# The experts' down product as three float32r matmuls with split weights, and two neighbouring weight rows to a partition

## The chip, the cores and the metric

The kernel runs on one core of a Trainium2 chip. The metric is the device time of one execution in microseconds (us), as the median of several runs. The engines are TensorE (PE in the profile, with its weight loads as PEld), VectorE (DVE), ScalarE (ACT), GpSimd (POOL) and SyncE (SP), which here issues most of the transfers.

## The reference, cut to what matters

One encoder layer over 1024 prompt and 256 sample tokens of 1024 features: two attentions, a gated merge, an output projection and a mixture of 32 experts, then a last norm. Everything is float32. The change lies in the experts:

```python
def hierarchical_moe(h, wg, bg, we, be, w1, w3, w2):
    ...
    def expert_block(args):
        xb, e = args
        return (jax.nn.silu(xb @ w1[e]) * (xb @ w3[e])) @ w2[e]
    ...
```

Each token goes to two of the 32 experts, so an expert has 80 tokens in the mean. `w1[e]` and `w3[e]` are 1024 x 512 and `w2[e]` is 512 x 1024, 2 MB each. The result is weighted, gated and added to the token's residual row.

## The kernel before

The expert stage takes the last third of the time. For each expert one block of up to 128 gathered token rows is worked on (`Block`): `xT` transposes the rows on TensorE, `up` makes the products with W1 and W3, `aT` transposes the activations, `down` makes the product with W2 and scatters the result back.

The loop over experts interleaves two experts on TensorE: the W1 product of expert e, the activation transposes of e - 1, the W3 product of e, the row transposes of e + 1, then the down product of e - 1. The order of the instructions on each engine is the order in which the program calls them, and each engine runs its own in order.

Products in float32r (a float32 rounded for one pass through TensorE) are made three at a time: high half by high half, low by high, high by low. For W1 and W3 `w_split` makes the halves of a 128 x 1024 quarter of the weights: ScalarE rounds it to the high half (line 1426), VectorE subtracts to get the low half (line 1427). The halves go to a ring of rooms of their own (`parts`, 2 * LEAD + 2 = 8 rooms of 4 KB a partition, four quarters). `w_next` hands out the next split quarter and has the one LEAD = 3 places further split. W2 isn't split: the down product reads the loaded quarters as float32 (line 1593), as it does the activations (`aT_`).

`w_load` loads a quarter from SyncE's queue into a free room, as far ahead as there are free rooms (`w_ahead`). Row r of a quarter of W1 or W3 goes to partition r mod 128, so a partition gets two runs of 2 KB, 128 rows apart; a W2 quarter has one row of 4 KB on each partition.

GpSimd issues the gather of the rows (line 1397) and the scatter that adds to the residual (line 1599). The rooms of `acts` hold a block's transposed rows and its output.

Of the kernel before, what the change touches and what calls it, by code (L numbers as in the profile page):

```python
# [10 lines left out]
F32 = mybir.dt.float32  # L11
# [22 lines left out]
class Slots:  # L34
    """4 KB rooms (1024 words a partition), given out in the order in which they fell free"""
# [4 lines left out]
    def ring(self, n):  # L40
        """n rooms set apart for one use"""
        return deque(self.free.popleft() for _ in range(n))
# [14 lines left out]
class Fm:  # L57
    """feature tiles of all tokens, chunk by chunk; rooms are taken when first touched"""
# [4 lines left out]
    def at(self, j, c, tok=None):  # L63
        """feature tile j of a chunk; tok: of one 128-token tile of it"""
        w = CHUNKS[c][1]
        per = 1024 // w
        o = (j % per) * w
        if (c, j // per) not in self.t:
            self.t[c, j // per] = self.s.get(self.dt)
        t = self.t[c, j // per]  # L70
        return t[:, o:o + w] if tok is None else t[:, o + tok * 128:o + tok * 128 + 128]
# [15 lines left out]
def kernel(ctx, tc, A, out_p, out_s, upto=99, dbg=None):  # L87
# [20 lines left out]
    def rsqrt(y, v, t):  # L108
        """y = v ** -0.5: square root and reciprocal, then a Newton step; t: room like y"""
# [6 lines left out]
    # scratch; a leading 2 where hi and lo parts lie side by side  # L116
# [40 lines left out]
    class Cols:  # L157
        """a group of up to 256 columns of w_in"""
# [29 lines left out]
    # column groups in the order of their use; gates only of the tokens behind the first chunk here  # L188
# [8 lines left out]
    # shift and scale of the first norm  # L197
# [36 lines left out]
    # norm statistics, then the normalised rows, transposed  # L234
# [46 lines left out]
    def ada0(hf):  # L281
# [12 lines left out]
        # norm_mix_g * (1 + scale): [p, hf, q, i, r], feature tile j = hf * 4 + q * 2 + i  # L294
# [17 lines left out]
    # the first column group runs feature tile by feature tile behind the modulation  # L312
# [30 lines left out]
    # the rest of the modulation, a piece at a time between projections  # L343
# [30 lines left out]
    def split_out(p, m, c, dst, row0, scale=1.0):  # L374
        """hi and lo of a PSUM (or SBUF) tile to scratch"""
# [13 lines left out]
    def work(g, *after):  # L389
        """the product with a loaded column group, then other parts; the next group's weights are split  # L390
        meanwhile, those of the one after are loaded"""
# [15 lines left out]
    def fm(g, evac, m=128, chunks=(0, 1, 2)):  # L407
        """feature-major column tile: out[m, tokens]"""
# [32 lines left out]
    # latents  # L441
# [69 lines left out]
    def rope(p, m, c, scale, dst, row0):  # L511
        """positions restart at the sample group"""
# [104 lines left out]
    def bias_out():  # L617
        """relative column bias of every query and key column"""
        SY.dma_start(tz_d, raw_ap(A["rpb"], 63, [[127, 120], [-1, 64], [1, 64]]))

    def bias_tables():
        """column bias of the neighbourhood attention by row distance, window-masked; the second table is of
        query tiles whose neighbourhoods lie inside the grid; a stage of each of three heads at a time"""
# [31 lines left out]
    class Piece:  # L655
        """[128, 8, 128] of weights: eight row tiles of 128 columns"""
# [24 lines left out]
    def piece_gates():  # L681
        """logits of the first chunk's gates"""
# [29 lines left out]
    class Merge:  # L712
        """per-branch projections and the gated merge, feature-major; the weights serve the first and the last
        chunk at once, then the middle one"""
# [95 lines left out]
    def fill(n):  # L810
        """up to the n-th product in all; a finished sum leaves its bank before the next begins"""
# [5 lines left out]
    def ktile(srcs):  # L817
        """a tile of hi or lo parts; srcs: (first partition, rows, dram)"""
# [6 lines left out]
    def heads(ap, rows, h0, nh, t0, w):  # L825
        """rows of each of nh heads, [rows, head, tokens]"""
        return ap[h0 * rows:(h0 + nh) * rows, t0:t0 + w].rearrange("(h d) n -> d h n", h=nh)

    class Job:
        """what a pair of heads (prompt) or two pairs (sample) need on chip"""  # L830
# [34 lines left out]
        def bias(b, h):  # L865
            if b.g:
                # two heads to a room, the rows that two query tiles reach
# [19 lines left out]
    class Unit:  # L887
        """a head's 128 queries"""
# [17 lines left out]
        def scores(u):  # L906
            """the score blocks, a bank each"""
# [34 lines left out]
        def transpose(u, b):  # L942
            """normalised P with the keys on partitions, in P's own place"""
# [12 lines left out]
    def pv(a, b):  # L956
        """both heads' values for one query tile"""
# [30 lines left out]
    for i in range(2):  # L988
# [5 lines left out]
        # two queries' pair of one kind, then of the other  # L994
# [48 lines left out]
    # logits = (x1 * rs * G2 + sh2) @ w + b = (x1 @ (G2 * w)) * rs + (sh2 @ w + b), features on partitions  # L1043
# [91 lines left out]
    # sum of the two column groups of the router's product  # L1135
# [30 lines left out]
    def rows_load(g):  # L1166
        """gate of the residual, shift, norm_ffn_g * (1 + scale), on all partitions"""
# [28 lines left out]
    # constants: column indices, token numbers (from 1), strict prefix matrix  # L1196
# [6 lines left out]
    # column indices less 64, so that the least number among zeros elsewhere is a column's  # L1203
# [6 lines left out]
    # of each token's two experts: number, place in the expert's list, weight  # L1210
# [231 lines left out]
    def w_next(e, m, q):  # L1442
        """the next quarter of the stream: of W1 and W3 split, LEAD quarters behind it are split before it is used"""
        if m == 2:
            return loaded.pop((e, m, q))
# [325 lines left out]
```

## Time and profile before

| what | before |
|---|---|
| median of 3 runs | 1901.58 us (1895.93 to 1902.13) |
| profiled execution, first to last instruction | 1893.6 us |
| TensorE busy | 1786.4 us (94%) |
| VectorE, ScalarE, GpSimd busy | 1034.4, 858.3, 328.9 us |
| expert stage in the profile | about 1235 to 1852 us |
| transfers in the expert stage | about 360 GB/s |

The time of a run also holds what lies before the first and after the last instruction; for the profiled execution itself only the span is known, and the runs lie 2.3 to 8.5 us above it. TensorE's busy time counts a matmul until its modelled end, so it overlaps with the next one's.

### The profile page before, as it was taken

The numbers are of one execution on the slowest core, as the hardware profiler recorded it, in microseconds if no ns is written. First come the engines' busy times: TensorE is split into PE (matmuls) and PEld (weight loads), VectorE is DVE, ScalarE is ACT, GpSimd is POOL, SyncE is SP. The second block draws the span as 40 slices with busy tenths as digits, with TensorE's granted clock in tenths as the row PEclk, the third lists the DMA queues.
The fourth block names the chain that finished last, engine by engine and source line by source line (L and its number), as shares of the span: only waits on it lengthen the run. The fifth ranks groups of instructions, "written<-read, shape, count | busy, mean of one in ns | idle before, by whom it ended". The sixth has DMA issues, their size and how long they took to land.

```text
span 1893.6 us, 28088 instructions
## 1 busy us (share of the span) xinstructions
PE 1786.4 (94%) x10298; PEld 1395.5 (74%) x10298; DVE 1034.4 (55%) x1739; ACT 858.3 (45%) x1392; POOL 328.9 (17%) x329
## 2 busy tenths in 40 slices
PE   5999999998999999989899999699999999999991
PEld 4777778997888888778688878566766667676760
DVE  6324422221455555444446566677777777777764
ACT  5313222221455555656633222265565656565642
POOL 0010210000222222222423100111111111111110
PEclk9999999999999999999999999799999999999996
DMA  9237787757632454755996553999999999999916
GB/s 352 92 113 214 239 277 219 225 167 209 141 100 63 118 155 120 218 156 157 272 312 205 189 211 132 347 340 369 365 365 361 354 366 353 364 356 367 348 37 238
DMA packets 294451, 453.85 MB, mean 240 GB/s; under 512 B 54711, under 2 KB 154119, under 8 KB 294311
## 3 DMA queue, kind: packets, MB, share of 16 engines
q1 hardware_dynamic: 277607, 403.77, 64.0%
q0 software_dynamic: 13824, 37.77, 7.2%
q10 hardware_dynamic: 2880, 10.49, 1.4%
q8 instruction: 83, 1.36, 0.3%
q14 instruction: 57, 0.47, 0.1%
HBM read 375.82 MB, written 90.67 MB: 246 GB/s over the span
## 4 chain that ended last, share of the span: by engine, by line
PE 85%; DVE 4%; DMA 4%; issue 3%; ACT 2%; SPq 1%; POOL 0%; DVEq 0%; POOLq 0%; ACTq 0%; another core or an unknown queue 0%
PE ph L1567 18%; PE pg L414 14%; PE py L1593 11%; PE s L918 6%; PE pw L1330 5%; PE fp L781 5%; PE o L968 5%; PE tp L950 5%; PE fp L693 4%; PE pg L576 3%; PE pt L1554 1%; PE pg L329 1%; PE pg L534 1%; DMA gate_d<-s 1%; DMA s<-nak_d 1%
## 5 line engine op out<-in xcount | busy, mean ns | idle before, releaser
L1567 PE MATMUL ph<-s,s 128*128 128x512 f32 x1536 | 377.9, 402 | 1.5 <-DVE s L1557 1.2
L1426 ACT CAST s<-s 128x1024 fp32r<-128x1024 f32 x256 | 265.9, 1055 | 195.0 <-PE ph L1567 195.0
L1567 PEld LDWEIGHTS ph<-s,s 128*128 128x128 f32 x1536 | 287.1, 189 | 73.9 <-issue 13.9
L1427 DVE TENSOR_TENSOR s<-s,s 128x1024 fp32r<-128x1024 f32 x256 | 304.6, 1222 | 64.5 <-ACT s L1426 55.2
L414 PE MATMUL pg<-s,s 128*128 128x512 f32 (+1 forms) x1488 | 284.5, 352 | 7.2 <-ACT s L176 6.0
L414 PEld LDWEIGHTS pg<-s,s 128*128 128x128 f32 (+1 forms) x1488 | 235.1, 186 | 57.5 <-ACT s L176 6.8
L1593 PE MATMUL py<-s,aT 128*128 128x512 f32 x512 | 225.1, 593 | 0.7 <-ACT aT L1582 0.7
L940 POOL TENSOR_SCALAR s<-s,m 128x1024 f32<-128x1024 f32 (+3 forms) x160 | 133.1, 832 | 472.1 <-DVE m L939 370.3
L1593 PEld LDWEIGHTS py<-s,aT 128*128 128x128 f32 x512 | 94.9, 190 | 108.1 <-issue 94.4
L918 PE MATMUL s<-s,s 96*128 96x512 f32 (+4 forms) x656 | 158.7, 365 | 1.4 <-ACT s L936 1.4
L936 ACT ACTIVATE s<-s,m 128x1024 f32<-128x1024 f32 (+3 forms) x160 | 135.1, 844 | 48.2 <-DVE m L926 27.2
L952 ACT COPY s<-tp 128x512 f32<-128x512 f32 (+1 forms) x160 | 86.7, 542 | 135.4 <-PE tp L950 132.8
L918 PEld LDWEIGHTS s<-s,s 96*128 96x128 f32 (+1 forms) x656 | 118.8, 190 | 27.3 <-ACT s L936 2.1
L950 PE MATMUL tp<-ident,s 128*128 128x128 f32 (+1 forms) x864 | 123.8, 276 | 11.4 <-POOL s L940 5.9
L693 PE MATMUL fp<-s,s 128*128 128x512 f32 x384 | 127.3, 432 | 0.3 <-ACT s L697 0.2
L950 PEld LDWEIGHTS tp<-ident,s 128*128 128x128 f32 (+1 forms) x864 | 101.7, 141 | 29.2 <-POOL s L940 10.6
L1330 PE MATMUL pw<-s,s 128*128 128x512 f32 x480 | 118.5, 402 | 0.0
L968 PE MATMUL o<-s,s 128*64 128x128 f32 (+1 forms) x1728 | 116.9, 281 | 0.2 <-ACT s L952 0.2
L177 DVE TENSOR_TENSOR s<-s,s 128x1024 fp32r<-128x1024 f32 (+1 forms) x32 | 38.3, 1200 | 143.2 <-ACT s L176 139.2
L781 PE MATMUL fp<-s,s 128*128 128x512 f32 (+1 forms) x576 | 112.4, 356 | 2.7 <-DVE s L670 1.0
L926 DVE TENSOR_REDUCE m<-s 128x1 f32<-128x1024 f32 (+1 forms) x80 | 85.0, 1062 | 51.3 <-PE s L918 50.8
L1599 POOL DMA_INDIRECT x_d<-s,idx x32 | 71.8, 2243 | 231.1 <-DVE s L1598 122.6
(227 smaller groups left out, 2041.7 us busy)
## 6 DMA issues: line engine op xcount, KB each, us to landing
s<-in_expert_w SPq DMA_DIRECT2D x384, 512.0 KB
s<-in_w_in SPq DMA_DIRECT2D x47, 512.0 KB
s<-in_ada_w POOLq DMA_DIRECT2D x32, 512.0 KB, 6.3
s<-nak_d SPq DMA_DIRECT2D x40, 256.0 KB
s<-in_x_prompt SPq DMA_DIRECT2D x16, 512.0 KB
s<-in_ada_w SPq DMA_DIRECT2D x16, 512.0 KB
s<-gate_d SPq DMA_DIRECT2D x16, 512.0 KB
gate_d<-s SPq DMA_DIRECT2D x16, 384.0 KB
```

The lines of the kernel that those rows point to most:

```text
L414: PE.matmul(p[:m, :CHUNKS[c][1]], g.at(a, j, 0, m), b.at(j, c), start=(j == 0 and n == 0), stop=(j == KD - 1 and n == 2))
L693: PE.matmul(p, w.at(a, j), b.at(j, 0), start=(n == 0), stop=(n == 23))
L781: PE.matmul(p[:, :w], b.ws[i].at(u, x * 4 + j), o[:, v, :w], start=(m == 0), stop=(m == 11))
L918: PE.matmul(u.s[:, b, :u.w], a, c, start=(n == 0), stop=(n == len(ops) - 1))
L936: S.activation(u.out, u.src, AF.Exp, bias=u.m[:, 0:1], scale=u.sign, accum_out=u.m[:, 1:2])
L950: PE.transpose(tp[:w, i // 128, :], u.P[:, b * 512 + i:b * 512 + i + w], ident)
L968: PE.matmul(o[64 * u.x:64 * u.x + 64, cs], u.job.vat(u.t0 + i // 128, u.h, w), v3(u.P, 8)[:w, i // 128, :], start=(i == 0), stop=(i + 128 ...
L1330: PE.matmul(b.p, x[b.c].at(k, b.c, b.k), w[:, k % 2, :], start=(k + i == 0), stop=(k == 7 and i == 2))
L1426: S.copy(hi, r)
L1427: V.tensor_sub(lo, r, f32(hi))
L1567: PE.matmul(p, a[:, 2 * q + k, :], v3(w, 2)[:, k, :], start=(q + k + i == 0), stop=(q == 3 and k == 1 and i == 2))
L1593: PE.matmul(p, b.aT_[:, k, :], w[:, hb * 512:hb * 512 + 512], start=(k == 0), stop=(k == 3))
```

## The change

The stream that `w_next` and `w_fill` walk through now holds the W2 quarters too: each is split like those of W1 and W3, with the subtraction on GpSimd (`G`) where it was on VectorE (`V`) for the others. `aT` makes a high and a low half of the transposed activations, in a room of `acts`, which has 4 rooms in place of 3. `down` makes three float32r matmuls for each quarter and half of the columns in place of one in float32; the third of the three reads the low half of the weights.

All loads now put row 2p and row 2p + 1 of a W1 or W3 quarter on partition p, one run of 4 KB. So that the rows of the gathered block meet the right weight rows, `xT` transposes every second column.

The loop for further blocks of experts with more than 128 tokens is changed in the same way; it makes no turn with these inputs. Comments and docstrings are left out of the new file, with the line numbers kept; they are left out here too.

```diff
-    LEAD, ACTS = 3, 3
+    LEAD, ACTS = 3, 4
...
-        SY.dma_start(v3(r, k), src.rearrange("(k p) n -> p k n", p=128)[:, q * k:q * k + k, :])
+        SY.dma_start(v3(r, k), src.rearrange("(q p k) n -> q p k n", p=128, k=k)[q])
         return r
 
-    def w_split(r):
+    def w_split(r, m):
         hi, lo = sl.get(F32R, parts), sl.get(F32R, parts)
         S.copy(hi, r)
-        V.tensor_sub(lo, r, f32(hi))
+        (V if m < 2 else G).tensor_sub(lo, r, f32(hi))
         sl.put(r)
         w_ahead(0)
         return hi, lo
 
     loaded, ready = {}, deque()
-    halves = [k for k in stream if k[1] < 2]
...
     def w_next(e, m, q):
-        if m == 2:
-            return loaded.pop((e, m, q))
-        assert halves[at[2]] == (e, m, q)
+        assert stream[at[2]] == (e, m, q)
         at[2] += 1
         w_fill()
         return ready.popleft()
 
     def w_fill():
-        while at[1] < min(len(halves), at[2] + LEAD):
-            ready.append(w_split(loaded.pop(halves[at[1]])))
+        while at[1] < min(len(stream), at[2] + LEAD):
+            ready.append(w_split(loaded.pop(stream[at[1]]), stream[at[1]][1]))
             at[1] += 1
...
                 for k in range(4):
-                    PE.transpose(p[:, k, :], b.xg[:, (hb * 4 + k) * 128:(hb * 4 + k) * 128 + 128], ident)
+                    o = (hb * 2 + k // 2) * 256 + k % 2
+                    PE.transpose(p[:, k, :], b.xg[:, o:o + 255:2], ident)
...
-            b.aT_ = ep.tile([128, 4, 128], F32, name="aT")
-            S.copy(b.aT_, p)
+            b.aHL = sl.get(F32R, acts)
+            b.aH, b.aL = [v3(b.aHL, 8)[:, 4 * i:4 * i + 4] for i in range(2)]
+            S.copy(b.aH, p)
+            V.tensor_sub(b.aL, p, f32(b.aH))
...
             for k in range(4):
-                w = quarter(2, k)
-                for hb, p in enumerate(ps):
-                    PE.matmul(p, b.aT_[:, k, :], w[:, hb * 512:hb * 512 + 512], start=(k == 0), stop=(k == 3))
-                sl.put(w)
-                w_ahead(0)
+                hi, lo = quarter(2, k)
+                for i, (a, w) in enumerate(((b.aH, hi), (b.aL, hi), (b.aH, lo))):
+                    for hb, p in enumerate(ps):
+                        PE.matmul(p, a[:, k, :], w[:, hb * 512:hb * 512 + 512], start=(k + i == 0), stop=(k == 3 and i == 2))
+                sl.put(hi, lo)
+            sl.put(b.aHL)
...
-        quarter = lambda m, q: w_split(raws[m, q]) if m < 2 else raws[m, q]
+        quarter = lambda m, q: w_split(raws[m, q], m)
```

## Rows read from the trace of the kernel before

**Rows 1.** The page: engines, busy us, share of the span, instructions.
```profile
PE 1786.4 (94%) x10298; PEld 1395.5 (74%) x10298; DVE 1034.4 (55%) x1739; ACT 858.3 (45%) x1392; POOL 328.9 (17%) x329
```
**Rows 2.** The chain that ended last, one expert: start us, us, what.
```profile
1435.21 6.87 PE py L1593 x16
1442.08 5.50 PE ph L1567 x24
1447.58 0.44 PE pt L1580 x4
1448.02 5.48 PE ph L1567 x24
1453.49 0.87 PE pt L1554 x8
```
**Rows 3.** Two stretches (engines' busy us, clock, DMA, GB/s); SP's wait, 1300 to 1780.
```profile
1550.00:1600.00 50.00, 50.00 (x192) 33.55 (x191) 36.08 (x38) 28.23 (x33) 10.02 (x6) 1.00 1.01 364
...
1815.00:1820.00 5.00, 5.00 (x24) 3.60 (x23) 5.00 (x6) 3.72 (x6) 0.00 (x0) 1.00 0.00 0
...
SPq L1421 <- DVE s L1427: 204.2, 197, 3.0
```
**Rows 4.** Groups by line, 1300 to 1800: busy us, mean ns of one, idle before.
```profile
L1427 DVE TENSOR_TENSOR s<-s,s 128x1024 fp32r<-128x1024 f32 x209 | 248.9, 1222 | 51.7 <-ACT s L1426 43.2 <-DMA s<-in_expert_w 5.0
L1426 ACT CAST s<-s 128x1024 fp32r<-128x1024 f32 x208 | 216.3, 1056 | 165.1 <-PE ph L1567 165.1
...
L1599 POOL DMA_INDIRECT x_d<-s,idx x26 | 59.9, 2304 | 172.3 <-DVE s L1598 92.8 <-DMA s<-h_d,idx 79.5
...
L1557 DVE TENSOR_TENSOR s<-pt,s 128x512 fp32r<-128x512 f32 x53 | 34.0, 683 | 0.0
L1588 DVE SCALAR_TENSOR_TENSOR s<-s,of,s 128x1024 f32<-128x1024 f32 x26 | 33.4, 1285 | 0.7
...
L1397 POOL DMA_INDIRECT s<-h_d,idx x27 | 28.0, 1037 | 248.1 <-PE pt L1554 248.1
...
L1572 ACT ACTIVATE a<-ph 128x512 f32<-128x512 f32 x26 | 15.5, 597 | 14.0 <-PE ph L1567 14.0
```
**Rows 5.** Groups by line of GpSimd over the whole span, the same columns.
```profile
L1354 POOL TENSOR_TENSOR s<-s,s 128x1024 f32<-128x1024 f32 x2 | 4.7, 2337 | 37.1 <-PE pr L1386 37.1
...
L520 POOL TENSOR_TENSOR s<-s 128x256 f32<-128x256 f32 x2 | 1.5, 734 | 5.0 <-issue 5.0
```
**Rows 6.** Timelines, 1197 to 1212: start us, us, what, idle before.
```profile
1197.69 0.69 DVE L1336 TENSOR_TENSOR s<-s,s 128x512 f32<-128x512 f32 x1
...
1209.02 2.34 POOL L1354 TENSOR_TENSOR s<-s,s 128x1024 f32<-128x1024 f32 x1 [32.34 <-PE pr L1386]
1209.41 2.49 DVE L1336 TENSOR_TENSOR s<-s,s 128x512 f32<-128x512 f32 x1
```
**Rows 7.** Timeline at 965 us.
```profile
964.90 1.21 DVE L670 TENSOR_TENSOR s<-s,s 128x1024 fp32r<-128x1024 f32 x1
965.06 1.65 POOL L791 TENSOR_TENSOR s<-s 128x256 f32<-128x256 f32 x1 [9.58 <-DVE s L790]
```
**Rows 8.** Timeline of VectorE within one expert.
```profile
1507.13 4.63 DVE L1427 TENSOR_TENSOR s<-s,s 128x1024 fp32r<-128x1024 f32 x4 [1.33 <-ACT s L1426]
...
1537.03 1.61 DVE L1598 SCALAR_TENSOR_TENSOR s<-py,slots,s 128x512 f32<-128x512 f32 x2 [3.01 <-PE py L1593]
```
**Rows 9.** One stretch: TensorE busy second, granted clock third from the end.
```profile
1248.00:1252.00 4.00, 2.55 (x13) 1.76 (x12) 4.00 (x6) 2.23 (x4) 1.28 (x1) 1.00 0.94 361
```
**Rows 10.** The end: one row of the chain, then the timeline.
```profile
1836.77 6.88 PE py L1593 x16
...
1843.47 0.60 PE L1580 MATMUL pt<-ident,a 128*128 128x128 f32 x4
1844.17 0.58 ACT L1582 COPY aT<-pt 128x512 f32<-128x512 f32 x1 [10.09 <-PE pt L1580]
1844.80 7.13 PE L1593 MATMUL py<-s,aT 128*128 128x512 f32 x16 [0.73 <-ACT aT L1582]
```

## Prediction

> **What bounds the kernel now.** I read the engine shares first, then the chain that ended last, then the waits of the expert stage alone. The shares only say that TensorE is busy nearly throughout [rows 1]. The chain is what to look at: through the whole expert stage it stays on TensorE and repeats every 19.16 us, which is one expert. Its pieces are 24 matmuls of a block's W1 product (5.50), four transposes (0.44), 24 of W3 (5.48), eight transposes (0.87) and the 16 records of the down product of the expert before (6.87); 5.50 + 0.44 + 5.48 + 0.87 + 6.87 = 19.16 [rows 2]. There is no piece of another engine in it, so a quarter's halves are always ready in time. The transfers are near their limit but not on the path: 364 GB/s in a typical 50 us, yet the queue that issues them spends 204 of 480 us waiting for VectorE to have read a room alone, and by 1815 us nothing is loaded any more while TensorE computes until 1852 [rows 3, 10].
>
> **What TensorE gains.** A float32r matmul costs 5.50 / 24 = 0.229 us. The down product is 8 calls (four quarters, two halves of the columns), shown as 16 records of 6.87 / 16 = 0.429. It becomes 24 float32r matmuls, as many as W1 has: 5.50 in place of 6.87, 1.37 less per expert. With nothing else late an expert would take 17.78 us, 32 x 1.37 = 44 us less in all. That is the gain on offer.
>
> **What the splits cost.** Each W2 quarter now needs a cast on ScalarE (1.056, four per expert) and a subtraction on GpSimd. ScalarE was busy 28.23 of 50 us, 10.8 per expert; with 4 x 1.056 it comes to 15.0, under 17.78 and so no bound by itself [rows 3, 4]. The new 128x512 subtraction for the lower half of the activations reads PSUM and SBUF like L1557: 0.68 on VectorE [rows 4].
>
> GpSimd's price is shown by the one instruction of this shape, two 128x1024 float32 inputs in SBUF: 2.337 us, both times; the 128x256 form of L520 at 0.73 is in line with that [rows 5]. Nothing in a rounded output suggests a different price: on VectorE the shape costs 1.222 with a rounded output (L1427) [rows 4]. So I take 2.34, and 4 x 2.34 = 9.35 us of GpSimd per expert. The Trainium skill (GPSIMD Engine Reference, 3.1 Elementwise — side-by-side cycle accounting) measures 4497 ns at twice the elements; half of that, an estimate, is 2.25, and the sum below would be 4 x 0.09 = 0.36 less per expert, some 11 us in all. The row decides.
>
> **GpSimd and VectorE exclude each other.** This is what decides the case, and the trace has it in both directions. At 1209.02 GpSimd starts its 2.34 us; VectorE's L1336, a 128x512 with both inputs in SBUF, starts at 1209.41 and lasts 2.49 until 1211.90, against 0.69 when alone at 1197.69: it ran only when GpSimd had ended at 1211.36 [rows 6]. The other way round, L791 on GpSimd started at 965.06, inside VectorE's L670 (964.90 to 966.11), and ended 0.60 after it, having taken 1.65 where the 128x256 shape takes 0.73 [rows 5, 7]. The one that waited lost its start only once: 0.60 of 0.73 and 0.54 of 0.69 were left, so a handover hides about 0.14. The Trainium skill (SBUF — State Buffer, Who interferes with whom) has the rule: a VectorE instruction with two SBUF inputs and a GpSimd instruction that reads SBUF share a port, and the second blocks until the first has finished. Read strictly, it hides no start, and the period below would be 0.7 longer; the rows hide 0.14 each, and I follow them.
>
> So what counts is what needs that port per expert: eight VectorE subtractions of W1 and W3 (1.22), L1588 (1.285) and the four on GpSimd [rows 4, 5]: 9.76 + 1.29 + 9.35 = 20.4 us, or 19.6 with six handovers taken off. That is already above today's 19.16, in whatever order they come.
>
> **The order makes it longer.** Splits run three quarters ahead in a ring of four quarters' rooms. Take as zero the end of GpSimd's subtraction for the last W2 quarter of an expert. VectorE has by then done one W1 quarter of the next expert at most, because GpSimd held the port. It now owes, in its program order, W1 q1 and q2, the two evictions of the down product (1.61 the pair, [rows 8]), W1 q3, W3 q0 to q2, the activations' lower half (0.68) and W3 q3. Four subtractions in a row take 4.63, so a further one costs (4.63 - 1.22) / 3 = 1.14 [rows 8]. Seven at 1.14 to 1.22, 8.0 to 8.5, plus 1.61 and 0.68: 10.3 to 10.8 us. Only then does GpSimd get the port for W2 q0. Then come its four subtractions, 9.35. L1588 slips in between (1.29); so do the next gather's issue, which waits in GpSimd's queue ahead of the last subtraction (1.04, [rows 4]), and beside it VectorE's first W1 quarter (1.22, the longer). That is 11.9, less five handovers of 0.14: 11.2. Together 21.5 to 22.0; I take 21.7. TensorE's 17.78 fits inside, with 3.9 idle per expert, by this order in stretches of about 2 us before the last third of W2 q2 and q3: only the two matmuls of a quarter that read its rest wait. A stall of that size cost no clock before: TensorE was busy 2.55 of 4 us at 1248 and kept 1.00 [rows 9].
>
> **Lower bound: no exclusion.** Without it there still is a ring of dependencies. After the last W1 matmul ScalarE must run the SiLU (0.60), the copy of the transposed activations (0.58) and two casts (2 x 1.06) [rows 4, 10] before GpSimd can start, with some 0.25 for four hand-offs, an estimate from the 0.05 to 0.1 us that lie between the transposes, their copy and the matmul behind it at 1844: 3.5. Then four GpSimd subtractions and the gather, 10.4; two matmuls of the last quarter and its hand-off, 0.56; the next W1, 5.50. That is 20.0, +0.8 against 19.16. The upper bound hides no starts and spaces VectorE's subtractions at 1.22: 22.0 + 0.7, 22.7, +3.5.
>
> **The rest.** W1 and W3 rows: 256 runs of 2 KB become 128 of 4 KB per load. Loads are not waited for, so this is worth nothing now, nor in the forecast, which moves the same bytes in more time. The transposes of the gathered rows read every second column: nothing if the weight load doesn't mind, at most their own 0.87 per expert if it takes twice as long, hidden in TensorE's 3.9 idle. W2's raw rooms are held until GpSimd has read them; SP's queue of loads waits for that, but with a lead of 40 us. The scatter (2.3, [rows 4]) stands in GpSimd's queue ahead of the next expert's first W2 subtraction; it goes out behind the evictions, some 4 us after zero, and has ended well before the 10.3. One room less for weights (ACTS 4) only trims the lead.
>
> **The sum.** 30 periods between down products: 30 x 2.55 = 76.5. The last one has no W1 and W3 beside it: four GpSimd subtractions follow each other with a scatter's issue (2.3) ahead of the last, and 1.0 to finish: 9.35 + 2.3 + 1.0 = 12.7, where the trace has 1836.77 to 1844.80, 8.0, before [rows 10]: +4.7. The fill at the start: 0 to 1. Total +82, bounds 30 x 0.8 + 3 = +27 and 30 x 3.5 + 5 = +110. The profiled span of 1893.6 would become 1976. The timed runs lie 2.3 to 8.5 us above that span; their median of 1901.58 becomes 1983. For this kernel 0.3% is 6 us, about what a measurement can tell from no change.
>
> **Rivals.** (a) The splits keep up and TensorE's gain is kept: -44, 1858. This needs a GpSimd subtraction short enough: by the sum above the period equals 19.16 at 2.34 - 2.55 / 4 = 1.70 us, and below that the kernel is faster. For it: both rows of 2.337 are with an unrounded output. Against: 0.73 at 256 columns already allows little under 2.3 [rows 5]. 6%. (b) The splits keep up but the loads don't: 364 GB/s x 19.16 us is 6.97 MB per expert, and at 17.78 that is 392 GB/s, which no 50 us stretch here shows. Then nothing changes: 1902, with 1896 to 1908. Against: it needs (a) first. 4%. The Trainium skill (DMA: Bandwidth & Descriptors, Specifications) gives about 358 GB/s of HBM per core, under which no gain could come of a faster TensorE at all; the trace's 364 is already over it. (c) The exclusion binds less than I say, since GpSimd's turns fall into VectorE's PSUM work (L1557, L1574) or its idle time: +6 to +55, worked out as the 20.0 above: about 1929. 20%. (d) My forecast, +55 to +112: 66%. (e) TensorE's clock falls in the new idle stretches, or GpSimd and VectorE trade turns badly: over +112, 4%.
>
> **Chances and range.** Faster is (a), 0.06; same is (b), 0.04; slower (c) to (e), 0.90. The range runs from 1920, which cuts off the first 12 of (c)'s 49 us, some 5 in 100, to 2013, the end of (d); with (a), (b) and (e) 19 in 100 are left out.
>
> **What would show it.** In the changed kernel's profile: the chain leaves TensorE and alternates between VectorE's L1427 successors and GpSimd; down products start about 21.7 us apart; GpSimd's 128x1024 subtractions have a mean of 2.3 or more (their waiting is counted in), and those VectorE subtractions that fell behind GpSimd last 2 us and more, so the group's mean rises well above 1.22; TensorE's down product has 24 matmuls of 0.23 with gaps of about 2 us ahead of the last two in a quarter; GB/s falls to about 320. I'd be wrong if GpSimd's subtraction took under 1.7, if VectorE's kept 1.22 beside it, or if the chain stayed on TensorE.

## Result and the profile after

The changed kernel takes 2013.4 us (median of 4 runs, 2007.59 to 2018.47) against 1900.9 for the kernel before in the same session: the ratio is 1.059, with an interval of 1.057 to 1.062. The forecast was 1983 with a range up to 2013. The sign was right, and so was the place where TensorE waits; the loss is 112 us where 82 were forecast.

The page of the changed kernel, engine shares as in [rows 1]. GpSimd's busy time has doubled, TensorE's has grown by 19 us although the down product got cheaper:

```profile
PE 1805.1 (90%) x10554; PEld 1471.6 (73%) x10554; DVE 1153.0 (57%) x1771; ACT 982.3 (49%) x1520; POOL 662.0 (33%) x457
```

Groups by line of the changed kernel, 1300 to 1900, the columns of [rows 4]:

```profile
L1427 DVE TENSOR_TENSOR s<-s,s 128x1024 fp32r<-128x1024 f32 x214 | 309.2, 1483 | 20.2 <-ACT s L1426 19.4
...
L1427 POOL TENSOR_TENSOR s<-s,s 128x1024 fp32r<-128x1024 f32 x107 | 257.6, 2427 | 124.5 <-ACT s L1426 118.5 <-PE ph L1566 5.2
...
L1589 DVE SCALAR_TENSOR_TENSOR s<-s,of,s 128x1024 f32<-128x1024 f32 x26 | 64.3, 2474 | 6.5 <-ACT s L1588 6.5
L1601 POOL DMA_INDIRECT x_d<-s,idx x27 | 62.1, 2302 | 108.8 <-DVE s L1600 108.8
L1397 POOL DMA_INDIRECT s<-h_d,idx x26 | 47.4, 1823 | 3.8 <-issue 0.8 <-PE py L1595 0.5
```

GpSimd's subtraction has a mean of 2.43, near the 2.34 of [rows 5]. VectorE's same line has gone from 1.22 to 1.48, and L1589, the old L1588, from 1.285 to 2.47 [rows 4]: they wait for GpSimd inside their own time. The issue of the gather takes 1.82 instead of 1.04. GpSimd's subtractions were held up by ScalarE's casts (118.5 us) and its scatters by VectorE's evictions (108.8), not by a full queue.

The waits of the changed kernel, 1300 to 1900 (total, times, longest):

```profile
POOL s L1427 <- ACT s L1426: 118.5, 26, 6.2
...
PE py L1595 <- POOL s L1427: 71.0, 28, 2.8
...
ACT s L1555 <- DMA x_d<-s,idx: 23.2, 12, 3.3
```

TensorE now waits once per expert for the rest of W2's last quarter, 2.7 to 2.8 us in most of them. The timeline of the changed kernel shows one turn of the ring (start us, us, what, idle before and its releaser):

```profile
1511.19 0.60 ACT L1571 ACTIVATE a<-ph 128x512 f32<-128x512 f32 x1 [0.56 <-PE ph L1566]
...
1511.68 0.58 ACT L1582 CAST s<-pt 128x512 fp32r<-128x512 f32 x1
1512.15 3.06 ACT L1426 CAST s<-s 128x1024 fp32r<-128x1024 f32 x3
...
1514.30 7.16 POOL L1427 TENSOR_TENSOR s<-s,s 128x1024 fp32r<-128x1024 f32 x3 [6.15 <-ACT s L1426]
...
1521.61 1.85 POOL L1397 DMA_INDIRECT s<-h_d,idx  x1
...
1523.49 2.38 POOL L1427 TENSOR_TENSOR s<-s,s 128x1024 fp32r<-128x1024 f32 x1
...
1525.93 1.22 PE L1595 MATMUL py<-s,s 128*128 128x512 f32 x2 [2.77 <-POOL s L1427]
...
1526.95 8.03 PE L1566 MATMUL ph<-s,s 128*128 128x512 f32 x24
```

Read it as a circle: the SiLU after W1, the copy of the activations, the casts, three subtractions on GpSimd, the gather's issue, the fourth subtraction, two matmuls, the next W1, the next SiLU. That is the prediction's "Lower bound: no exclusion", link for link; no instruction of VectorE is one of its links, though VectorE's work lengthens the gather's issue. But W1 takes 8.03 here, where its 24 matmuls took 5.50 before [rows 2].

Why it does is in the windows of the changed kernel, one per expert (start:end, length, TensorE's busy us, the other engines', then granted clock, DMA share, GB/s). Of these eight, two turns are at full clock:

```profile
1443.20:1464.20 21.00, 18.23 (x86) 14.70 (x85) 17.07 (x15) 15.19 (x17) 13.69 (x6) 1.00 0.91 309
1464.20:1487.15 22.95, 20.18 (x85) 15.76 (x84) 18.19 (x16) 15.17 (x17) 13.87 (x6) 0.93 0.92 322
1487.15:1511.00 23.85, 21.10 (x86) 16.77 (x85) 18.38 (x17) 15.15 (x17) 13.69 (x6) 0.86 0.91 305
1511.00:1534.80 23.80, 21.04 (x85) 16.78 (x84) 18.24 (x16) 15.16 (x17) 13.69 (x6) 0.86 0.88 291
...
1579.66:1600.64 20.98, 18.22 (x85) 14.71 (x84) 17.00 (x15) 15.19 (x17) 13.69 (x6) 1.00 0.89 307
```

TensorE's idle time is the same in all of them: 21.00 - 18.23 = 2.77, 23.80 - 21.04 = 2.76. What differs is its busy time for the same matmuls, 18.2 or up to 21.1, and with it the granted clock. The same view in 4 us steps, for the turn at 1511 and for the one at 1580, shows where:

```profile
1520.00:1524.00 4.00, 3.16 (x14) 2.11 (x12) 4.00 (x3) 3.47 (x4) 3.82 (x3) 1.00 0.76 229
1524.00:1528.00 4.00, 2.07 (x5) 1.69 (x6) 4.00 (x2) 1.04 (x1) 1.87 (x1) 0.66 0.67 197
1528.00:1532.00 4.00, 4.00 (x11) 3.10 (x10) 3.68 (x5) 1.17 (x2) 2.30 (x1) 0.50 1.00 392
1532.00:1536.00 4.00, 4.00 (x21) 3.29 (x20) 2.45 (x2) 2.97 (x5) 0.00 (x0) 0.99 1.00 293
...
1592.00:1596.00 4.00, 1.40 (x6) 1.18 (x7) 4.00 (x3) 1.25 (x2) 2.52 (x2) 1.00 0.69 216
1596.00:1600.00 4.00, 4.00 (x20) 3.29 (x19) 4.00 (x5) 2.86 (x3) 1.63 (x1) 1.00 0.93 346
```

After the wait of 2.77 us the granted clock is 0.50, the lower of TensorE's two levels (1.2 GHz), and TensorE gets 11 matmuls into 4 us where 20 go at full clock. After an equal wait at 1592 it keeps 1.00. So the same stall sometimes costs only itself and sometimes as much again.

The account, from the starts of the activation transposes (1262.34 to 1936.03 here, 1255.92 to 1830.70 before): 30 periods of 22.46 instead of 19.16, 98.9 us more. Of these, (21.0 - 19.16) x 30 = 55 are the ring at full clock and (22.46 - 21.0) x 30 = 44 the clock. The step to the last of those transposes adds 1950.96 - 1936.03 against 1843.47 - 1830.70, 2.2 us, and what follows 4.7. The remaining 6.4 lie ahead of the first of those transposes; 5.9 of them were there before the stage of the experts began. Together 112.2, the difference of the profiled spans (2005.8 and 1893.6). The window over the thirty periods bears the 44 out:

```profile
1262.34:1936.03 673.69, 590.81 (x2524) 469.19 (x2522) 534.42 (x454) 454.99 (x510) 411.83 (x183) 0.93 0.87 293
```

TensorE is busy for 590.8, which is 44 more than 30 x 18.22, and idle for 82.9, which is 30 x 2.76.

### The profile page after: what moved, and what is told of

It reads as the page before. It is cut to its first block, busy times and chain, and to the rows that moved or that the text cites. A ratio compares the mean times of both kernels' runs of the same rounds, so it can differ in the third digit from the quotient of the medians.

```text
span 2005.8 us, 29229 instructions
## 1 busy us (share of the span) xinstructions
PE 1805.1 (90%) x10554; PEld 1471.6 (73%) x10554; DVE 1153.0 (57%) x1771; ACT 982.3 (49%) x1520; POOL 662.0 (33%) x457
## 5 line engine op out<-in xcount | busy, mean ns | idle before, releaser
L1426 ACT CAST s<-s 128x1024 fp32r<-128x1024 f32 x384 | 390.3, 1053 | 162.0 <-PE ph L1566 98.0
L1566 PE MATMUL ph<-s,s 128*128 128x512 f32 x1536 | 402.6, 422 | 3.6 <-DVE s L1427 2.3
L1427 DVE TENSOR_TENSOR s<-s,s 128x1024 fp32r<-128x1024 f32 x256 | 366.7, 1471 | 26.6 <-ACT s L1426 25.4
L1566 PEld LDWEIGHTS ph<-s,s 128*128 128x128 f32 x1536 | 313.0, 206 | 78.0 <-DVE s L1427 5.2
L1427 POOL TENSOR_TENSOR s<-s,s 128x1024 fp32r<-128x1024 f32 x128 | 311.8, 2456 | 145.2 <-ACT s L1426 139.1
L1595 PE MATMUL py<-s,s 128*128 128x512 f32 x768 | 205.5, 413 | 88.1 <-POOL s L1427 86.4
L1595 PEld LDWEIGHTS py<-s,s 128*128 128x128 f32 x768 | 139.1, 192 | 138.6 <-POOL s L1427 111.4
L950 PE MATMUL tp<-ident,s 128*128 128x128 f32 (+1 forms) x864 | 123.8, 276 | 11.6 <-POOL s L940 6.3
L950 PEld LDWEIGHTS tp<-ident,s 128*128 128x128 f32 (+1 forms) x864 | 101.6, 140 | 29.7 <-POOL s L940 11.6
```

The lines of the kernel that those rows point to most:

```text
L950: PE.transpose(tp[:w, i // 128, :], u.P[:, b * 512 + i:b * 512 + i + w], ident)
L1426: S.copy(hi, r)
L1427: (V if m < 2 else G).tensor_sub(lo, r, f32(hi))
L1566: PE.matmul(p, a[:, 2 * q + k, :], v3(w, 2)[:, k, :], start=(q + k + i == 0), stop=(q == 3 and k == 1 and i == 2))
L1595: PE.matmul(p, a[:, k, :], w[:, hb * 512:hb * 512 + 512], start=(k + i == 0), stop=(k == 3 and i == 2))
```

## Experiments

Three theories were carried through the runs. **Exclusion**: the port that VectorE and GpSimd share sets the period, as forecast. **Ring**: GpSimd's latency, between W1 and the next W1, makes TensorE wait, and then its clock falls. A third came in with the misses: the **output room**, an SBUF room that the next writer can only have when a scatter has landed.

**The layout alone.** W1 and W3 two neighbouring rows to a partition with the strided transposes; the down product as before.

```diff
-        SY.dma_start(v3(r, k), src.rearrange("(k p) n -> p k n", p=128)[:, q * k:q * k + k, :])
+        SY.dma_start(v3(r, k), src.rearrange("(q p k) n -> q p k n", p=128, k=k)[q])
...
+                    o = (hb * 2 + k // 2) * 256 + k % 2
+                    PE.transpose(p[:, k, :], b.xg[:, o:o + 255:2], ident)
```

> The kernel before with the two-row layout of W1 and W3 and the strided transposes alone; the down product stays in float32. Both theories: nothing waits for the loads and TensorE does the same matmuls, so 1901 us within 6. If the strided reads of the transposes cost their own 0.87 us per expert, +28 us; if wider runs of 4 KB mattered, a gain.

Measured: 1902.0, ratio 1.002 (1.001 to 1.003), every period 19.22 instead of 19.16. The transposes' weight loads take 206 ns instead of 140; no other change was found. As both theories expected, the layout is not the cause; the loss lies in the down product.

**Filling TensorE's wait.** Ten further matmuls that nobody reads, ahead of the two that wait.

```diff
                 for i, (a, w) in enumerate(((b.aH, hi), (b.aL, hi), (b.aH, lo))):
+                    if k == 3 and i == 2:
+                        pd = psh.tile([128, 512], F32, name="pd")
+                        for _ in range(10):
+                            PE.matmul(pd, b.aH[:, k, :], hi[:, 0:512], start=True, stop=True)
```

> The changed kernel with ten matmuls more per expert, 2.3 us, whose result nobody reads, placed in TensorE's wait ahead of the last two matmuls of each down product. Ring theory (the period is a ring of GpSimd's four subtractions and the gather's issue, two matmuls, the next W1 product and ScalarE's four steps, 21.0 us at full clock, and the clock's falls after the waits of 2.7 us add 1.5 in the mean): the clock stays at 1.00, every period becomes about 21.0 and the time falls by some 44 us to about 1970, although TensorE does more. Exclusion theory (the port that VectorE and GpSimd share sets the period): TensorE isn't on the path, 2013 us within 10.

Measured: 1980.2, ratio 1.044 (1.042 to 1.046). TensorE does 73 us more work (10 x 32 x 0.229) and the kernel is 33 us faster than the changed one. The ring theory had said 1970. Periods are 21.0 to 22.3, most of them 21.2 to 21.6, and in the windows of this run from 1500 to 1528 the granted clock is 1.00 in all seven; two of them:

```profile
1500.00:1504.00 4.00, 3.62 (x16) 2.67 (x15) 3.75 (x4) 4.00 (x5) 3.82 (x3) 1.00 0.88 353
1504.00:1508.00 4.00, 3.47 (x15) 2.55 (x14) 4.00 (x2) 1.11 (x3) 2.00 (x1) 1.00 0.64 182
```

Nothing of VectorE's or GpSimd's work was touched, so exclusion predicted no change. The mean period is 21.52, 0.94 less than the changed kernel's 22.46: with the clock at 1.00 from 1300 to 1850, this run gives back 28 of the 44 us above 21.0 per expert. The other 0.5 per expert stays here at full clock; what it is was not looked for.

**The gather behind the last subtraction.** GpSimd's queue then has four subtractions in a row.

```diff
                 hi, lo = quarter(2, k)
+                if k == 0 and then is not None:
+                    then.gather()
```

> The changed kernel with the issue of the next gather moved in GpSimd's queue from ahead of the last W2 subtraction to behind it. Ring theory: 1.85 us leave the ring, TensorE's wait shrinks from 2.7 to about 1 us, the clock holds, the period comes to 19.3 to 20.0: 1915 to 1935 us. Exclusion theory: the port has the same work, only the W1 subtraction that ran beside the gather moves: 1990 to 2013 us.

Measured: 1972.8, ratio 1.039 (1.037 to 1.041): 41 us better than the changed kernel, but neither theory's number. Periods are 20.7 to 23.4, half of them 21.2; TensorE's longest wait is 1.7. By the ring theory some 1.85 should have left each period. Something new ends the idle time of ScalarE, in the waits of this run, 1300 to 1900:

```profile
ACT s L1555 <- DMA x_d<-s,idx: 60.3, 24, 4.5
```

L1555 copies the next expert's gathered rows; it waits for a scatter to land, because its room was the last output's. This is the first sign of the output room.

**Six rooms in place of four**, in the changed kernel and with the late gather.

```diff
-    LEAD, ACTS = 3, 4
+    LEAD, ACTS = 3, 6
```

> The changed kernel with six rooms for the rows in place of four and nothing else. Theory A (TensorE waits for GpSimd's last rest of a quarter, the clock falls in that wait, and the rooms are a minor matter): of the 23 us that ScalarE waited for a scatter to land at most those 23 come back, 1985 to 2013, with waits of 2.7 us for GpSimd's rest and a clock of about 0.95 as before. Theory R (the rooms are the root, as in the run with W2 on VectorE): the long periods of 22.3 to 24 go and all are near 21.0, 1950 to 1965.

> The late gather with two more rooms for activations and outputs, so that the copy of the next rows' transposes no longer waits for the last scatter to land (it did 60 us in all with the late gather alone, whose period was 21.2). Ring theory without a port limit: ScalarE's steps 3.3, four subtractions of GpSimd 9.4, two matmuls 0.6, the W1 product 5.5: 18.9, below the 19.16 of before; 1895 to 1905 us. Port theory: VectorE's backlog behind GpSimd decides as soon as the scatter doesn't, period 21 to 21.6, 1955 to 1980 us.

Measured: the changed kernel with six rooms 2005.5, ratio 1.056 (1.053 to 1.058), the clock at 0.948 and TensorE's waits for GpSimd unchanged at 71.5 us. So in the changed kernel the rooms are a minor matter: the 8 us lie within the two intervals. With the late gather 1970.4, ratio 1.037 (1.035 to 1.040), as without the rooms, while ScalarE's waits for scatters shrink from 60.3 to 13.4 us. That is in the port theory's 1955 to 1980 and far from the ring theory's 1895 to 1905. The timeline of the run with the late gather and six rooms shows where the 1.85 went:

```profile
1391.78 11.02 POOL L1427 TENSOR_TENSOR s<-s,s 128x1024 fp32r<-128x1024 f32 x4 [2.96 <-ACT s L1426]
```

Four subtractions in a row take 11.02, where the changed kernel has 7.16 + 2.38 = 9.54. L1589 on VectorE used to run beside the gather; now it takes its turn ahead of GpSimd's fourth subtraction, and the first of the four waits for a subtraction of VectorE. So GpSimd's latency sets the ring, and exclusion is part of that latency: it took back 1.5 of the 1.85.

**GpSimd that writes but hardly reads.** The rest of W2 is left zero, but for its first eight columns (the low half of W2 is left out of the product); GpSimd's time per quarter stays about the same.

```diff
-        (V if m < 2 else G).tensor_sub(lo, r, f32(hi))
+        if m < 2:
+            V.tensor_sub(lo, r, f32(hi))
+        else:
+            G.tensor_scalar(lo[:, 0:8], f32(hi)[:, 0:8], 0.0, None, op0=OP.mult)
+            for c0, c1 in ((8, 1024), (8, 1024), (8, 200)):
+                G.memset(f32(lo)[:, c0:c1], 0.0)
```

> The changed kernel with each W2 subtraction on GpSimd replaced by instructions of about the same total length (8 columns computed from the high half, then memsets over the rest), which read no second operand and almost nothing of SBUF; the low half of W2 is zero, so that part of the product is left out. Exclusion theory: VectorE and GpSimd no longer block each other, VectorE's subtractions return to 1.22 and the period to about 20.0: 1925 to 1945 us. Ring theory: GpSimd takes as long as before in the ring, only some 0.3 us of blocking per expert goes: 1990 to 2010 us.

Measured: 2030.7, ratio 1.069 (1.067 to 1.071), slower than the changed kernel and above both theories' ranges. Groups by line of this run, 1300 to 1900:

```profile
L1428 DVE TENSOR_TENSOR s<-s,s 128x1024 fp32r<-128x1024 f32 x204 | 245.3, 1224 | 64.0 <-ACT s L1426 44.6 <-POOL s L1432 11.1 <-DMA s<-in_expert_w 6.3
...
L1594 DVE SCALAR_TENSOR_TENSOR s<-s,of,s 128x1024 f32<-128x1024 f32 x25 | 32.1, 1286 | 6.3 <-ACT s L1593 6.3
```

VectorE is not held up at all, 1.224 and 1.286 as in the kernel before [rows 4], and still nothing is won. GpSimd's turn had become longer, 13.2 us with the gather in place of 11.6, TensorE waited 3.1 to 4.2 us in each expert, and the mean granted clock of 1300 to 1850 was 0.93. What VectorE loses to GpSimd was therefore not what set the period; the run can't say what an equally long turn without blocking would have given. The Trainium skill (SBUF — State Buffer, Who interferes with whom) says that a VectorE instruction with two SBUF inputs contends with a GpSimd instruction that reads SBUF and not with one that only writes. The trace agrees: 1.483 beside the subtractions, 1.224 beside the fills.

**All of W2's subtractions on VectorE**, first with four rooms, then with six, then with two of six for the output rows alone. The first line of the edit is in all three runs, the others in the third.

```diff
-        (V if m < 2 else G).tensor_sub(lo, r, f32(hi))
+        V.tensor_sub(lo, r, f32(hi))
...
-            y = sl.get(ring=acts)
+            y = sl.get(ring=ys)
...
-    parts, acts = sl.ring(2 * LEAD + 2), sl.ring(ACTS)
+    parts, acts, ys = sl.ring(2 * LEAD + 2), sl.ring(ACTS), sl.ring(2)
```

> The changed kernel with the four W2 subtractions on VectorE too, GpSimd left with its two transfers. Both theories: no blocking and no slow link in the ring, but VectorE gets 12 subtractions of 1.2, and with its other work some 19.9 us per expert: it becomes the bound, period 19.8 to 20.1, 1920 to 1932 us. It prices GpSimd's part: what it is faster than the changed kernel's 2013 is what the use of GpSimd for the subtraction costs.

> All of W2's subtractions on VectorE, as in the earlier run of that kind (2016.6, period about 23.5), but with six rooms for the rows in place of four, so that the copy of the next gathered rows doesn't wait for a scatter to have landed. Theory R (what cost the earlier run was the room that a scatter frees late, and then the clock that fell in the waits behind it): that wait goes, the period is set by VectorE's own queue at 19.8 to 20.2, TensorE's clock stays near 0.97, 1920 to 1935. Theory V (VectorE is simply too slow with twelve subtractions, or GpSimd's scatter blocked by them is the cost): the scatter's issue still takes 5.7 and the time stays at 2000 to 2020.

> All of W2's subtractions on VectorE with six rooms, as in the run before (1991.2), but two of the six now belong to the down product's output rows alone, so that an expert's output never takes the room that the scatter of the expert before it is still reading. Theory R (that room was what the period waited for, and the clock fell in the waits): ScalarE's waits for the scatter go; VectorE's own work is 518 us in 27 experts of the last trace, 19.2 each, and now sets the period at 19.3 to 20.0; 1905 to 1930, clock 0.97. Theory V (the scatter's issue of 5.7 us and TensorE's waits for the casts are the cost, wherever the output lies): 1975 to 1995 as before.

Measured: 2016.6 (ratio 1.062, 1.060 to 1.064), 1991.2 (1.049, 1.047 to 1.051), and 1882.6 (0.991, 0.989 to 0.994). The first two were misses of both theories; the third, faster than either theory said, shows why. The waits of the run with six rooms, 1300 to 1900, and then the timeline of the run with rooms for the output:

```profile
ACT s L1588 <- DMA x_d<-s,idx: 101.8, 27, 4.6
...
PE py L1595 <- ACT s L1426: 65.1, 27, 3.2
```

```profile
1519.65 4.62 DVE L1427 TENSOR_TENSOR s<-s,s 128x1024 fp32r<-128x1024 f32 x4
1520.01 5.71 POOL L1601 DMA_INDIRECT x_d<-s,idx  x1 [8.22 <-DVE s L1600]
...
1529.53 1.16 ACT L1588 ACTIVATE s<-s,of 128x1024 f32<-128x1024 f32 x1
...
1531.12 1.28 DVE L1589 SCALAR_TENSOR_TENSOR s<-s,of,s 128x1024 f32<-128x1024 f32 x1
```

Rooms are handed on in the order in which they were freed, four are taken per expert, and with six of them each output takes exactly the room of the output before it. Its first writer, L1588 on ScalarE, then waits for that scatter to land; the cast of W2's last quarter queues behind it, TensorE waits for that cast, and the clock falls (0.96 in the mean from 1300 to 1850). With rooms of their own L1588 waits for nothing, and 109 us come back, by three edited lines. Every period from the second to the twenty-ninth is 18.52 to 18.55, and VectorE is the bound: in the windows view of this run it is busy 40.00 of 40.00 us from 1500 to 1540.

**The same rooms with GpSimd's subtractions**, splits four quarters ahead, the gather late.

```diff
-    LEAD, ACTS = 3, 4
+    LEAD, ACTS = 4, 6
```

> The same with the splits four quarters ahead in place of three (two more rooms for halves), which takes ScalarE's steps out of the ring. Ring theory without a port limit: TensorE's 17.8 to 17.9 per expert, 1860 to 1870 us. Port theory: eight VectorE subtractions, L1589 and four of GpSimd can't run beside each other, 19.6 to 20.4 per expert at the least, 20.7 by a schedule written out with the trace's durations: 1940 to 1960 us, and VectorE's subtractions still last 1.4 us and more in the mean.

> The changed kernel with the gather issued behind the last subtraction, splits four quarters ahead, and two rooms for the output rows alone (the run without the last took 2003.4, period 22.4, with ScalarE waiting 122 us for scatters). The theory of the prediction (the shared port: what needs it adds up to 20.4 per expert, 19.6 with handovers taken off, whatever the order): no period under 19.6, 1920 to 1950. Theory G (GpSimd's own queue is full: four subtractions of 2.4 or more, a gather of 1.9, a scatter of 5.7): 22 again, 1995 to 2010. Theory R (neither, only latencies round a ring, which a lead of four takes away): 17.9 to 18.6, 1855 to 1885.

In the second, ACTS is back at 4 and the output has two rooms, as above. Measured: 2003.4 (1.055, 1.052 to 1.057), a miss of both theories, and 2005.6 (1.055, 1.052 to 1.058). Here the output room is worth nothing: ScalarE waited 122 us for scatters in the first, not in the second, and the time is the same. The timeline of the second tells what does bind once the ring has slack:

```profile
1523.17 4.62 DVE L1427 TENSOR_TENSOR s<-s,s 128x1024 fp32r<-128x1024 f32 x4
1527.71 1.40 DVE L1602 SCALAR_TENSOR_TENSOR s<-py,slots,s 128x512 f32<-128x512 f32 x2
1529.03 4.61 DVE L1427 TENSOR_TENSOR s<-s,s 128x1024 fp32r<-128x1024 f32 x4
1529.38 5.71 POOL L1603 DMA_INDIRECT x_d<-s,idx  x1 [5.22 <-DVE s L1602]
...
1534.57 9.98 POOL L1427 TENSOR_TENSOR s<-s,s 128x1024 fp32r<-128x1024 f32 x4
...
1538.30 7.34 DVE L1589 SCALAR_TENSOR_TENSOR s<-s,of,s 128x1024 f32<-128x1024 f32 x1 [0.25 <-ACT s L1588]
1544.71 1.86 POOL L1397 DMA_INDIRECT s<-h_d,idx  x1 [0.16 <-issue]
1545.56 1.21 DVE L1427 TENSOR_TENSOR s<-s,s 128x1024 fp32r<-128x1024 f32 x1
```

The two engines take turns in blocks. While VectorE runs eight subtractions GpSimd only ends a gather, waits for the evictions (L1602) and stands in its scatter; while GpSimd runs four, L1589 stands for 7.34 us, of which 1.285 is its work. From 1523.17 to 1545.56 that is a turn of 22.4, most periods of this run. This is the forecast's order sum (10.3 to 10.8 of VectorE, then 11.2) measured at 22.4 in place of 21.7: exclusion is real; as a bound of its own it stands behind the ring, and the changed kernel did not meet it. My theory of a full queue on GpSimd gave the number of this run, but GpSimd is not full: it is idle for 5.22 ahead of the scatter, and of the 5.71 of the scatter some 3.4 are more than the 2.30 that it takes in the changed kernel.

**Part of W2 only.** Two or three of the four quarters as split products on VectorE, the others in float32 as before, nothing on GpSimd, six rooms; then two quarters with the old layout; then three quarters with rooms for the output. NS is the number of split quarters.

```diff
+                if k >= NS:
+                    w = quarter(2, k)
+                    for hb, p in enumerate(ps):
+                        PE.matmul(p, b.aF[:, k - NS, :], w[:, hb * 512:hb * 512 + 512], start=False, stop=(k == 3))
+                    sl.put(w)
```

> Two of the four W2 quarters as three float32r matmuls with the subtractions on VectorE, the other two as one float32 matmul like before; nothing of it on GpSimd; ACTS 6. TensorE: 19.16 - 0.69 = 18.47 per expert. VectorE: 14.6 + 2 x 1.2 + 0.43 = 17.5, just under. Both theories: no shared port and no slow link, so TensorE stays the bound: period 18.5, about 1880 us, 1 per cent faster than before. If VectorE's order makes TensorE wait, 1890 to 1905.

> The version with two quarters of W2 split on VectorE, with W1 and W3 loaded as in the kernel before (two rows 128 apart to a partition) and the transposes of neighbouring columns. Theory L (the new layout only costs the slower transposes, 0.06 us per expert): period 18.47 instead of 18.53, 1876 to 1880. Theory M (the longer rows help the loads now that TensorE asks for them faster): the period is above 18.53 with waits for the loads, 1882 to 1900.

> Three of the four W2 quarters as three float32r products with the subtraction on VectorE, the fourth in float32, nothing of it on GpSimd, six rooms. Theory R (TensorE sets the period as long as VectorE's queue fits beside it): two quarters gave 18.53, a third takes another 0.34 off, 18.2, and 1868 to 1874. Theory V (the splits' latency catches up: the third quarter's subtraction stands behind the lower half of the activations and eight others): the period is 18.4 to 19.2 with waits of TensorE for VectorE's L1427, 1876 to 1900.

> Three quarters of W2 split on VectorE, the fourth in float32, as in the run before (1951.7, period 20.7: landing of a scatter 13.2, then 7.2 until the next one's issue), but with two of the six rooms for the output rows alone. Theory R: the ring of scatter, output room, evictions and scatter is gone, VectorE has 17.8 us of work per expert and TensorE 18.2, the period is 18.3 to 19.0, 1872 to 1895. Theory V (VectorE's subtractions come late for another reason): 20.0 or more, 1930 to 1955.

Measured: two quarters 1880.4 (0.990, 0.989 to 0.992), periods of 18.53; with the old layout 1879.3 (0.990, 0.988 to 0.991), periods of 18.45, so the layout's 0.06 to 0.08 per expert again. Three quarters with six rooms 1951.7 (1.028, 1.026 to 1.030), a miss, periods about 20.7; with rooms for the output 1882.7 (0.991, 0.990 to 0.993), periods 18.63. The chain that ended last, in the run with three quarters and six rooms, is the output room's ring in plain form (start us, us, what):

```profile
1505.91 13.20 DMA x_d<-s,idx
1519.11 0.02 issue
1519.14 0.02 POOLq L1614
1519.15 7.22 issue
1526.37 0.03 POOLq L1397
...
1526.61 12.86 DMA x_d<-s,idx
```

A scatter needs 13.2 us until it has landed, then 7.2 pass until the next one is issued; with the short steps between, 20.70 lie between two starts, whatever TensorE does. The four versions with no subtraction on GpSimd and no wait for a scatter's room are all about 1% faster than the kernel before; their intervals overlap, so none of them is shown to be the fastest. With two split quarters the output still takes the room of the output before it, but the scatter's issue takes 2.30 there, not 5.71, and ScalarE waits for no scatter.

## Why the prediction was wrong

- **TensorE's gain** (1.37 per expert) was right and is there to be had: with the subtractions on VectorE the same down product gives 18.53 per expert instead of 19.16, where VectorE is the bound.
- **ScalarE** at 15.0 per expert: 15.2 measured. **GpSimd's price** of 2.34: 2.43 measured. **GB/s** about 320: 282 to 324. **The layout** worth nothing: 1.002. **Loads** not waited for: no wait for the weights stands among the longer ones.
- **The wait's place and length** were nearly right: "stretches of about 2 us" ahead of the last two matmuls of a quarter; it is 2.77, once per expert, and only in the last quarter.
- **The step that failed** is "A stall of that size cost no clock before". It rested on one window [rows 9], 2.55 us busy of 4. The idle 1.45 there were not one wait but two, as the timeline of the kernel before has it:

```profile
1248.82 0.50 PE L1567 MATMUL ph<-s,s 128*128 128x512 f32 x1 [0.24 <-ACT s L1556]
1250.53 5.55 PE L1567 MATMUL ph<-s,s 128*128 128x512 f32 x23 [1.21 <-DVE s L1557]
```

  So the longest wait of that stretch was 1.21, less than half of 2.77. Here TensorE was busy 2.07 of 4 and the clock went to 0.50 behind it, but at another place it was busy 1.40 of 4 and kept 1.00. Over 30 experts the clock costs 44 us, two fifths of the loss, and the sum priced it at nothing; the rival (e) that named it had 4 in 100. The run with the ten filling matmuls shows it as a cause, by giving back 33 us for more work.
- **The path** was wrong too: "This is what decides the case" was said of exclusion. The period at full clock was given as 21.7 by exclusion's order and is 21.0 by the ring. That 30 x 2.55 = 76.5 came as near the measured 98.9 as it did is in part luck: 21 too much for the path, 44 too little for the clock. The ring's sum of 20.0 was worked out as a lower bound; it lacked 0.8 of the gather's issue, which takes 1.85 beside VectorE's subtractions instead of the 1.04 of [rows 4], and some 0.2 of GpSimd's longer subtractions. So VectorE's work enters this kernel as about 1 us on the ring. As a bound of its own it showed only when the ring had been given slack, at 22.4. By the ring alone the loss would have been some 55 + 7 us and the time about 1963, inside the range.
- **The signs** that were to show exclusion (subtractions of 2.3 and more on GpSimd, a mean well above 1.22 on VectorE, gaps ahead of the last two matmuls) came, for the two engines do exclude each other; but none of them says that this sets the period. Only "the chain leaves TensorE and alternates" between VectorE and GpSimd would have told the two apart, and the circle above has no such link.
- **The scatter** that "has ended well before the 10.3" had been issued by then, but lands 10.1 us after its issue; 23 us of waits for its room followed in the changed kernel. They were worth 8 us at most: the run with six rooms is not clear of the changed kernel by its interval. With W2 on VectorE, which the forecast didn't consider, the same room cost 109 us.
- **The end** was forecast at +4.7 and is +6.9, the fill at +0 to 1 and is +0.5 beside 5.9 that the profiled execution lost earlier.

Why the clock falls behind some waits of 2.77 us and not behind others stays open; no run varied it by itself. It does not come at random: from 1579.66 to 1804.99 the periods run 21.0, 23.0, 23.8, 22.3, 22.6 twice over. Shorter waits cost less often: with the late gather and six rooms, where TensorE's longest wait is 1.7, the clock is below 1.00 in six of the thirty periods, and with the filler, where no wait for GpSimd is longer than 0.74, in none. Why most of the late gather's periods are 21.23 and not 20.67 was not settled either.

## What to carry to other kernels

A stall on TensorE is to be priced twice, with and without the fall of the clock behind it, when the profile of before has no wait as long as the one to come. Before counting engines' work, follow the ring that a split closes: from the product that feeds it, over the slow engine, to the matmul that waits; work on an engine with half the speed costs by its latency there, not by its share of busy time. And a buffer that a scatter reads is busy until the scatter has landed: give outputs rooms of their own before concluding that an engine is too slow.

## What was not expected of the hardware

The issue of an indirect DMA on GpSimd is held up by VectorE's subtractions with two SBUF inputs. The gather's issue goes from 1.04, with none of them beside it in the kernel before, to 1.85. A scatter's issue that starts within such a subtraction takes 2.30 or 5.71. In the run with W2 on VectorE and output rooms it starts at 1520.01 within a block of four, 1519.65 to 1524.27, and ends 1.45 after the block. Its landing then goes from about 10 to 13 us, as the run with three quarters and six rooms shows.

Four subtractions in a row don't settle which of the two it is. The timeline of the changed kernel has the same block and the same start within it, 0.36 behind, and an issue of 2.31, which ends 1.46 after the first of the four (1.22 long):

```profile
1598.01 4.62 DVE L1427 TENSOR_TENSOR s<-s,s 128x1024 fp32r<-128x1024 f32 x4
1598.37 2.31 POOL L1601 DMA_INDIRECT x_d<-s,idx  x1 [3.82 <-DVE s L1600]
```

What decides whether the issue gets its turn after one subtraction or after four stays open.

In the run with a lead of four and output rooms VectorE doesn't get a turn between GpSimd's subtractions: L1589 stands for up to 7.34 us, with 1.285 of work. That is no fixed order: in the run with the late gather and six rooms, where GpSimd also runs four in a row, the same instruction takes 2.68 in the mean.
